# Two transformer blocks and two hybrid layers: inputs and output laid out by the host, x and the first weights loaded by pieces, and both heads' score banks filled in turn

## The chip, the cores and the metric

The kernel runs on one core of a Trainium2 chip. The metric is device time in microseconds (us), less is better. TensorE does matrix products and transposes, VectorE (DVE) and ScalarE (ACT) the elementwise work, GpSimd (POOL) little, and DMA transfers are issued from the queues of SyncE (SP) and ScalarE.

## What is computed

The input is x (256 tokens of 1024 features) and a memory of 256 tokens. A first model of two blocks is followed by a second one of two layers, all in float32. The first model, cut to its core:

```python
for i in range(DEPTH):                       # 2
    kvm = mem @ w_mem_kv[i]                  # 4 memory heads of 64
    if i % 2 == 0:
        proj = x @ w_in_swa[0]               # 12 heads, 3 key heads, window in chunks of 64
        self_out = swa_sink_attention(rope(q), rope(k), v, attn_sinks[0])
    else:
        proj = x @ w_in_fox[0]               # 12 heads, causal, bias cum[q] - cum[k]
        self_out = forgetting_attention(q, k, v, log_sigmoid(f_logit + b_forget[0]))
    cross_out = memory_attention(qc, km, vm)
    mix = concatenate([self_out, cross_out]) @ w_out[i]
    x = layer_norm(DN_ALPHA * x + mix, ln_attn_g[i], ln_attn_b[i])
    ffn = swiglu(x, ...) if i % 2 == 0 else moe_swiglu(x, ...)   # 8 experts, top 2
    x = layer_norm(DN_ALPHA * x + ffn, ln_ffn_g[i], ln_ffn_b[i])
```

The second model puts 16 meta tokens in front of the result and runs two layers. Each has a mixer (a gated delta rule with short convolutions beside an attention whose keys an indexer selects, then gates and an output product) and a convolutional gated MLP with D_FF 2816. The result is the 256 tokens without the meta tokens.

## The kernel before

Activations stand feature-major: partition = feature within a block of 128, then 8 blocks, then tokens. Every float32 number in the large products is cut into a high and a low part, and a product is three matmuls: high weight by high x (L228), high weight by low x (L229), low weight by high x (L230); L236 to L238 are the same with tokens on the output's partitions, L879 to L881 and L905 to L907 those of the experts. `linear` (L196) goes over groups of weight rows, `load_w` (L168) gets one: `fetch` (L165) puts a DMA of up to 1 MB on SP's queue into one of five buffers `raw`, ScalarE copies the high part `wh` (L179), VectorE subtracts for the low part `wl` (L182). The weights lie in memory as in the reference, so a transfer reads, for each partition, several strided rows.

The order within an engine's queue is fixed when the program is built, by a planner which goes by the order of the program text and by its own costs; each engine takes its queue strictly in that order.

At the start `consts` (L246) loads the constants `cst` by two DMAs on ScalarE's queue; `layer0` (L514) loads x token-major (`load_T`, L313: two DMAs of 512 KB on SP) and turns it (`turn`, L321): 16 transposes on TensorE (L327), a copy to float32 on VectorE (L331), the high part on ScalarE (L332), the low part on VectorE (L333). `rope1` (L335) makes the tables of sines; the rotation itself is a product with a constant matrix (L540). `vectors` (L259) loads the small vectors (gains, biases, convolution weights) row-wise by many DMAs on ScalarE's queue and turns them by TensorE (L278, L292, L303). `mem_tokens` (L488) loads and turns the memory like x.

`attend` (L421) handles two blocks b of two heads h at a time, in two halves t of the queries. For each t and h it takes one of two `sc` banks (each a PSUM bank); for each b a function `extra` puts a mask or bias into it (layer 0: L573, a product over 2 rows; layer 1: L667, a product over 44 rows with the cumulated gates, and L670, the causal mask), and the product of queries and keys over 64 rows is added (L434). A product with float32 operands is two records in the trace. Then the softmax: a maximum (L438) on VectorE, small operations, an exponential on ScalarE (L445) for each b, a scaling on VectorE (L453). The probabilities are transposed (L464), copied (L469 on ScalarE, L471 on VectorE) and multiplied with the values (L478); there the heads of a block write the two halves of the output's partitions, first all key tiles of one head, then those of the other. Head h=0 stands in partitions 0 to 63 of the queries and keys, h=1 in 64 to 127.

`moe` (L700) runs the router and 8 experts; a loop for tokens over the capacity follows it. `meta` (L955) loads the 16 meta tokens token-major and transposes them (L960). `consts2` (L926) loads the constants of the second model, among them `dtb` and `nA` (four small DMAs on SP, L947 and L948), and takes the exponential of the latter (L949), in ScalarE's queue beside the squares (L382) for the last norm of the first model. `gates` (L1224) loads 16 columns of w_in_2 as `ws` by two DMAs on SP. The last linear is the MLP's, with `ev` (L1093) adding its result to the stream h (L1094); then `store` (L963) transposes h (L970), copies it (L972, L974) and writes it by two DMAs of 512 KB (L975).

Of the kernel before, what the change touches and what calls it, by code (L numbers as in the profile page):

```python
# [105 lines left out]

class Kern:
# [88 lines left out]
    def linear(self, xs, w, c0, c, blocks, T, evac, tokmajor=(), accs=None, raws=None):  # L196
# [7 lines left out]
        wv = w.rearrange("(k p) c -> p k c", p=128)  # L204
# [12 lines left out]
        for k0, n in gs:  # L217
            wh, wl = self.load_w(wv[:, k0:k0 + n, ds(c0, c)], n, c)
# [39 lines left out]

    def vectors(self):  # L259
# [6 lines left out]
        I = self.i  # L266
        rows1 = [("ln_attn_g", 16), ("ln_attn_b", 16), ("ln_ffn_g", 16), ("ln_ffn_b", 16),
                 ("norm_mix_2", 16), ("norm_ffn_2", 16), ("b_gate_2", 32)]
        self.v = {}
        r = self.ap_.tile([128, T2], F, tag="sq", name="rows", bufs=2)[:, :128]  # L270
        o = 0
        vt = self.cp.tile([128, 128], F, name="vec1")
        for name, m in rows1:
            nc.scalar.dma_start(r[o:o + m, :], I[name].rearrange("l (k p) -> (l k) p", p=128))
            self.v[name] = vt[:, o:o + m].rearrange("p (l k) -> p l k", l=2)
            o += m
        p = self.pt()
        nc.tensor.transpose(p[:, :128], r, self.ident)  # L278
        nc.vector.tensor_copy(vt, p[:, :128])
# [3 lines left out]
        self.vn, self.convw, self.convf = {}, [], []  # L283
        r = self.ap_.tile([128, T2], F, tag="sq", name="rows", bufs=2)[:, :128]
        nc.vector.memset(r, 0.0)
        nc.scalar.dma_start(r[:96], I["conv_a_2"].rearrange("l i (k p) -> (l i k) p", p=128))
        for i, name in enumerate(("a_out_norm_2", "q_norm_2", "k_norm_2")):
            nc.scalar.dma_start(r[96 + 2 * i:98 + 2 * i], I[name])
        nc.scalar.dma_start(r[102:104, :64], I["kidx_norm_2"])
        vt = self.cp.tile([128, 128], F, name="vec2")  # L290
        p = self.pt()
        nc.tensor.transpose(p[:, :128], r, self.ident)  # L292
        nc.vector.tensor_copy(vt, p[:, :128])
        cv = vt[:, :96].rearrange("p (l i k) -> p l i k", l=2, i=4)
        self.convw = [cv[:, l] for l in range(2)]
        for i, name in enumerate(("a_out_norm_2", "q_norm_2", "k_norm_2", "kidx_norm_2")):
            self.vn[name] = vt[:, 96 + 2 * i:98 + 2 * i]
        vt = self.cp.tile([128, 2, 66], F, name="vec3")
        for l in range(2):
            r = self.ap_.tile([128, T2], F, tag="sq", name="rows", bufs=2)[:, :128]  # L300
            nc.scalar.dma_start(r[:66], I["conv_ffn_2"][l].rearrange("i (k p) -> (i k) p", p=128))
            p = self.pt()
            nc.tensor.transpose(p[:, :66], r[:66], self.ident[:66, :66])  # L303
            nc.vector.tensor_copy(vt[:, l], p[:, :66])
            self.convf.append(vt[:, l].rearrange("p (i k) -> p i k", i=3))
        self.sinks = self.cp.tile([128, 12], F, name="sinks")
        nc.scalar.dma_start(self.sinks, I["attn_sinks"].to_broadcast([128, 12]))
        self.brout = self.cp.tile([128, 8], F, name="brout")
        nc.scalar.dma_start(self.brout, I["b_router"].to_broadcast([128, 8]))
        self.bforg = self.cp.tile([12, 1], F, name="bforg")  # L310
        nc.scalar.dma_start(self.bforg, I["b_forget"].rearrange("o h -> h o"))

    def load_T(self, pool, src, name):  # L313
# [3 lines left out]
        for t in range(2):  # L317
            nc.sync.dma_start(raw[:, ds(t * D, D)], src[ds(t * 128, 128), :])
        return [raw[:, :D], raw[:, D:]]

    def turn(self, toks, xT, xh, xl):  # L321
        nc = self.nc
        for t, a in enumerate(toks):
            for g in range(2):
                p = self.pt()
                for b in range(4):
                    nc.tensor.transpose(p[:, ds(b * 128, 128)], a[:, ds((g * 4 + b) * 128, 128)], self.ident)  # L327
                pv = p.rearrange("p (b t) -> p b t", b=4)
                o = (slice(None), slice(g * 4, g * 4 + 4), ds(t * 128, 128))
                if xT is not None:  # L330
                    nc.vector.tensor_copy(xT[o], pv)  # L331
                nc.scalar.activation(xh[o], pv, AF.Copy)  # L332
                nc.vector.tensor_tensor(xl[o], pv, xh[o].bitcast(F), op=OP.subtract)  # L333
# [87 lines left out]
    def attend(self, pool, qs, ks, vs, outs, nk, extra=None, sink=None):  # L421
# [33 lines left out]
        for b in range(2):  # L455
# [32 lines left out]
    def mem_tokens(self, pool):  # L488
        toks = self.load_T(pool, self.i["mem"][0], "memt")
        m = self.pair(S)  # L490
        self.turn(toks, None, *m)
# [24 lines left out]
    def layer0(self):  # L516
# [3 lines left out]
        with tc.tile_pool(name="l0", bufs=1) as pool:  # L520
            toks = self.load_T(pool, I["x"][0], "xt")
            self.turn(toks, x, xh, xl)
# [6 lines left out]
            w = I["w_in_swa"][0]  # L529
# [84 lines left out]
    def layer1(self, x, xh, xl):  # L614
        nc, I, tc = self.nc, self.i, self.tc
        with tc.tile_pool(name="l1", bufs=1) as pool:
# [6 lines left out]
            wf = pool.tile([128, KB, 12], F, name="wf")  # L623
            nc.scalar.dma_start(wf, w[:, 2560:2572].rearrange("(k p) c -> p k c", p=128))
# [36 lines left out]
            for b0 in range(0, 6, 2):  # L661
# [4 lines left out]
                def extra(t, b, h, p, n):  # L666
                    nc.tensor.matmul(p, fselr[h * 64:h * 64 + 44, ds((2 * (b0 + b) + h) * 128, 128)],  # L667
# [1013 lines left out]
```

## Time and profile before

| | us |
|---|---|
| median of three runs | 2384.94 |
| lowest and highest | 2368.7, 2387.02 |
| the profiled execution | 2384.18 |
| its span | 2382.4 |

The profile is of one execution. Its times are within the span; 1.8 us lie around the span. An engine's queue is in order, so an instruction that waits holds all behind it. "PEclk" is the mean granted clock of TensorE, 1.00 being 2.4 GHz and 0.50 being 1.2 GHz. The ends of matmuls are modelled: two neighbours overlap by some hundredths of a microsecond as they are shown, and starts are the safer reading.

### The profile page before, as it was taken

How to read it: one execution, taken by the hardware profiler on the slowest of the kernel's cores; microseconds unless marked ns; L12 is line 12 of the kernel's file. 1: busy time of each engine (PE TensorE's matmuls, PEld its weight loads, DVE VectorE, ACT ScalarE, POOL GpSimd, SP SyncE). 2: the span in 40 equal slices, each digit the busy share in tenths (PEclk: the TensorE clock that was granted, in tenths of full speed). 3: DMA queues.
4: the chain of work that ended last, by engine and by line, in shares of the span. 5: the costliest groups of instructions: out<-in, count | busy, mean ns of one | idle time of the engine just before them, and what ended most of it. 6: DMA issues, size and time to landing. Idle time of an engine off the chain costs nothing. (4 is left out here: it accounts for less than half of the span.)

```text
span 2382.4 us, 37173 instructions
## 1 busy us (share of the span) xinstructions
PE 2296.6 (96%) x15054; PEld 2042.5 (86%) x15054; DVE 1695.8 (71%) x2645; ACT 1325.8 (56%) x1840; POOL 65.3 (3%) x110
## 2 busy tenths in 40 slices
PE   7989998998999999999999979999999999999999
PEld 7779998776888888888887768889999989899999
DVE  6565546546898888888888766776876565858764
ACT  4445435335776767767677565454554463555543
POOL 0000000000000000000000010000100000000000
PEclk9899998978999999999999979999999989999999
DMA  7225554334999999999999542224555522244653
GB/s 245 96 89 162 184 186 132 105 95 151 360 357 325 349 348 347 334 359 352 324 361 353 192 129 76 86 74 166 163 173 171 162 76 84 77 143 158 195 176 125
DMA packets 296260, 478.94 MB, mean 201 GB/s; under 512 B 14800, under 2 KB 160060, under 8 KB 296082
## 3 DMA queue, kind: packets, MB, share of 16 engines
q1 hardware_dynamic: 292224, 474.82, 58.6%
q8 instruction: 120, 1.97, 0.3%
q10 hardware_dynamic: 3714, 1.55, 0.3%
q14 instruction: 58, 0.48, 0.1%
q0 software_dynamic: 144, 0.13, 0.0%
HBM read 475.55 MB, written 1.05 MB: 200 GB/s over the span
## 5 line engine op out<-in xcount | busy, mean ns | idle before, releaser
L182 DVE TENSOR_TENSOR wl<-raw,wh 128x1024 fp32r<-128x1024 f32 (+2 forms) x565 | 882.4, 1573 | 295.9 <-ACT wh L179 293.8
L179 ACT ACTIVATE wh<-raw 128x1024 fp32r<-128x1024 f32 (+2 forms) x565 | 744.0, 1332 | 421.5 <-PE acc L229 248.4
L228 PE MATMUL acc<-xh,wh 128*128 128x272 f32 (+2 forms) x2224 | 645.2, 293 | 3.9 <-ACT qk L1120 1.8
L229 PE MATMUL acc<-xl,wh 128*128 128x272 f32 (+2 forms) x2224 | 646.6, 292 | 1.4 <-DVE xl L1043 1.1
L230 PE MATMUL acc<-xh,wl 128*128 128x272 f32 (+2 forms) x2224 | 644.2, 291 | 1.4 <-DVE wl L182 1.4
L228 PEld LDWEIGHTS acc<-xh,wh 128*128 128x128 f32 x2224 | 425.8, 193 | 9.9 <-ACT qk L1120 2.2
L229 PEld LDWEIGHTS acc<-xl,wh 128*128 128x128 f32 x2224 | 425.9, 192 | 8.1 <-issue 3.6
L230 PEld LDWEIGHTS acc<-xh,wl 128*128 128x128 f32 x2224 | 425.9, 192 | 4.1 <-DVE wl L182 2.1
L881 PE MATMUL acc<-wl,xe 128*128 128x512 f32 (+1 forms) x768 | 289.5, 378 | 3.0 <-DVE wl L182 3.0
L879 PE MATMUL acc<-wh,xe 128*128 128x512 f32 (+1 forms) x768 | 289.6, 377 | 0.0
L880 PE MATMUL acc<-wh,xe 128*128 128x512 f32 (+1 forms) x768 | 288.7, 376 | 0.0
L182 DVE TENSOR_TENSOR wl<-rawxl,wh 128x2048 fp32r<-128x2048 f32 x73 | 166.3, 2289 | 17.9 <-ACT wh L179 17.6
L881 PEld LDWEIGHTS acc<-wl,xe 128*128 128x128 f32 x768 | 144.3, 188 | 31.6 <-DVE wl L182 5.1
L879 PEld LDWEIGHTS acc<-wh,xe 128*128 128x128 f32 x768 | 144.8, 189 | 26.7
L880 PEld LDWEIGHTS acc<-wh,xe 128*128 128x128 f32 x768 | 144.3, 188 | 26.2
L179 ACT ACTIVATE wh<-rawxl 128x2048 fp32r<-128x2048 f32 x73 | 139.6, 1916 | 32.1 <-PE acc L906 15.6
L228 PE MATMUL acc<-gh,wh 128*128 128x256 f32 (+1 forms) x528 | 150.3, 285 | 0.0
L229 PE MATMUL acc<-gl,wh 128*128 128x256 f32 (+1 forms) x528 | 150.2, 285 | 0.0
L230 PE MATMUL acc<-gh,wl 128*128 128x256 f32 (+1 forms) x528 | 150.1, 284 | 0.0
L906 PE MATMUL acc<-wh,egl 128*128 128x512 f32 x352 | 139.4, 396 | 0.0
L905 PE MATMUL acc<-wh,egh 128*128 128x512 f32 x352 | 139.1, 395 | 0.0
L907 PE MATMUL acc<-wl,egh 128*128 128x512 f32 x352 | 132.8, 396 | 0.0
(554 smaller groups left out, 3022.7 us busy)
## 6 DMA issues: line engine op xcount, KB each, us to landing
raw<-in_w_exp_in_dram SPq DMA_DIRECT2D x125, 1024.0 KB, 6.0
raw<-in_w_exp_out_dram SPq DMA_DIRECT2D x64, 1024.0 KB, 7.0
rawxl<-in_w_exp_in_dram SPq DMA_DIRECT2D x49, 1024.0 KB, 5.8
raw<-in_w_up_dram SPq DMA_DIRECT2D x44, 1024.0 KB, 5.2
rawxl<-in_w_exp_out_dram SPq DMA_DIRECT2D x24, 1024.0 KB, 7.5
raw<-in_w_in_dram SPq DMA_DIRECT2D x24, 1024.0 KB, 5.4
raw<-in_w_ffn_in_dram SPq DMA_DIRECT2D x22, 1024.0 KB, 5.0
raw<-in_w_out_dram SPq DMA_DIRECT2D x16, 1024.0 KB, 5.0
```

The source lines that it names most:

```text
L179: nc.scalar.activation(h[:, o], raw[:, o], AF.Copy)
L182: nc.vector.tensor_tensor(l[:, o], raw[:, o], h[:, o].bitcast(F), op=OP.subtract)
L228: nc.tensor.matmul(o, f(wh[:, j]), xh[:, k], start=st, stop=False)
L229: nc.tensor.matmul(o, f(wh[:, j]), xl[:, k], start=False, stop=False)
L230: nc.tensor.matmul(o, f(wl[:, j]), xh[:, k], start=False, stop=sp)
L879: nc.tensor.matmul(a, xe[0][:, k], wh[:, q], start=k == 0, stop=False)
L880: nc.tensor.matmul(a, xe[1][:, k], wh[:, q], start=False, stop=False)
L881: nc.tensor.matmul(a, xe[0][:, k], wl[:, q], start=False, stop=k == KB - 1)
L905: nc.tensor.matmul(ys[h], gh[:, k], wh[:, q, o], start=k == 0, stop=False)
L906: nc.tensor.matmul(ys[h], gl[:, k], wh[:, q, o], start=False, stop=False)
L907: nc.tensor.matmul(ys[h], gh[:, k], wl[:, q, o], start=False, stop=k == FB - 1)
```

## The change

It rearranges what the host hands over and the order of some work; the products are the same.

- Weights: each group of rows that `load_w` asks for lies as one contiguous block in memory, partition by partition (`Packed`); the DMA has one run for each partition. The host makes the blocks.
- x and mem: handed over feature-major. x is loaded in four pieces of two blocks, with the two halves of the first weight tile in turn (`load_x`), and its parts are cut piece by piece; mem is one fetch and two cuts. The transposes go. The constants `cst` go to SP's queue, behind x and the first weights, as one DMA.
- Small vectors: one array made by the host, one DMA; the transposes go. Later parts of it (`late`) hold the forget gate's weights, the router's, the meta tokens and `ws`, each loaded by one DMA on ScalarE's queue where it is used. `dtb` and the logarithms for `nA` are in the part that is loaded at the start.
- `attend`: both heads' banks are taken together, `extra` is called once for each t and h with a product over both blocks where it can be, and the score products go through the blocks with the heads in turn. The products with v go through the key tiles with the heads in turn.
- Output: feature-major. Each block of 128 features (128 KB) is stored right after its last addition, straight from h; the host turns the result.

```diff
+class Packed:
...
+    def tile(self, l, k0, n, c0, c):
+        key = (k0, n, c0, c)
+        if key not in self.places:
+            self.places[key] = self.used
+            self.used += 128 * n * c
...
+        return self.ap[l, o:o + 128 * n * c].rearrange("o (p x) -> (o p) x", p=128)
...
     def fetch(self, src, kb, c, raw=None):
         raw = self.raw() if raw is None else raw
-        self.nc.sync.dma_start(raw[:, :kb * c].rearrange("p (k c) -> p k c", k=kb), src)
+        self.nc.sync.dma_start(raw[:, :kb * c], src)
...
-            wh, wl = self.load_w(wv[:, k0:k0 + n, ds(c0, c)], n, c)
+            wh, wl = self.load_w(w(k0, n, c0, c), n, c)
...
-        nc.scalar.dma_start(t[:, :128], self.cst_d[:, :128])
-        nc.scalar.dma_start(t[:, 128:], self.cst_d[:, 128:n])
+        self.cst = t
...
+        vt = self.cp.tile([128, n], F, name="vec")
+        nc.scalar.dma_start(vt, self.i["vec"][:, :n])
...
+    def late(self, pool, name):
+        a, w = self.i["off"][name]
+        t = pool.tile([128, w], F, name=name)
+        self.nc.scalar.dma_start(t, self.i["vec"][:, ds(a, w)])
+        return t.rearrange("p (k c) -> p k c", k=KB)
+
+    def load_x(self, x, xh, xl, w):
         nc = self.nc
         raw = self.raw()
...
+        for k in range(0, KB, 2):
+            o = slice(k, k + 2)
+            nc.sync.dma_start(x[:, o], self.i["x"][:, ds(k * S, 2 * S)].rearrange("p (k t) -> p k t", k=2))
+            if k < 4:
+                q = ds(k * 512, 1024)
+                nc.sync.dma_start(raw[:, q], w[:, q])
+        self.ahead.append(raw)
+        for k in range(0, KB, 2):
+            o = slice(k, k + 2)
+            self.split(xh[:, o], xl[:, o], x[:, o])
+        nc.sync.dma_start(self.cst, self.cst_d[:, :self.cst.shape[1]])
...
-            for h in range(2):
-                p = self.sc()
-                pv = p[:, :2 * n].rearrange("p (b k) -> p b k", b=2)
-                sl = slice(h * 64, h * 64 + 64)
-                for b in range(2):
-                    started = extra(t, b, h, pv[:, b], n) if extra else False
-                    nc.tensor.matmul(pv[:, b], qs[b][sl, ds(t * 128, 128)], ks(b, h)[:, :n],
-                                     start=not started, stop=True)
+            pvs = [self.sc()[:, :2 * n].rearrange("p (b k) -> p b k", b=2) for _ in range(2)]
+            if extra:
+                for h in range(2):
+                    extra(t, h, pvs[h], n)
+            for b in range(2):
+                for h in range(2):
+                    sl = slice(h * 64, h * 64 + 64)
+                    nc.tensor.matmul(pvs[h][:, b], qs[b][sl, ds(t * 128, 128)], ks(b, h)[:, :n],
+                                     start=b == 0 and not extra, stop=b == 1, skip_group_check=True)
+            for h, pv in enumerate(pvs):
...
             o = self.pt()
-            for h in range(2):
-                for kt in range(2):
-                    c0, t = segs[kt]
-                    n = (2 - t) * 128
+            for kt in range(2):
+                c0, t = segs[kt]
+                n = (2 - t) * 128
+                for h in range(2):
...
-            def extra(t, b, h, p, n):
-                nc.tensor.matmul(p, hmb[:, :128], hmb[:, ds(128 + t * 256, n)], start=True, stop=False)
-                return True
+            def extra(t, h, p, n):
+                nc.tensor.matmul(p, hmb[:, :128], hmb[:, None, ds(128 + t * 256, n)].to_broadcast([2, 2, n]),
+                                 start=True, stop=False, skip_group_check=True)
...
+                def extra(t, h, p, n):
+                    for b in range(2):
+                        nc.tensor.matmul(p[:, b], fselr[h * 64:h * 64 + 44, ds((2 * (b0 + b) + h) * 128, 128)],
+                                         cum[h * 64:h * 64 + 44, :n],
+                                         start=b == 0, stop=False, skip_group_check=True)
+                    nc.tensor.matmul(p[:, :, ds(t * 128, 128)], self.identb,
+                                     self.causb[:, None, :].to_broadcast([128, 2, 128]),
+                                     start=False, stop=False, skip_group_check=True)
...
-            nc.sync.dma_start(self.dtb[:, l], I["dt_bias_2"][l:l + 1].to_broadcast([128, 4]))
-            nc.sync.dma_start(self.nA[:, l], I["a_log_2"][l:l + 1].to_broadcast([128, 4]))
-        nc.scalar.activation(self.nA, self.nA, AF.Exp)
+        nc.scalar.activation(self.nA, al, AF.Exp)
...
-                if not l:
+                if l:
+                    nc.sync.dma_start(self.out[:, ds(k * S, S)], h[:, k, NM:])
+                else:
                     self.ready(h, k, self.v["norm_mix_2"][:, 1])
...
-        nc.sync.dma_start(ws[:, :, 0:8], wv[:, :, 2048:2056])
-        nc.sync.dma_start(ws[:, :, 8:16], wv[:, :, 3400:3408])
+        ws = self.late(pool, f"ws{l}")
```

## Rows read from the trace of the kernel before

**Rows 1.** The page: TensorE's share of the span, and traffic in 40 slices.

```profile
PE 2296.6 (96%) x15054; PEld 2042.5 (86%) x15054; DVE 1695.8 (71%) x2645; ACT 1325.8 (56%) x1840; POOL 65.3 (3%) x110
...
GB/s 245 96 89 162 184 186 132 105 95 151 360 357 325 349 348 347 334 359 352 324 361 353 192 129 76 86 74 166 163 173 171 162 76 84 77 143 158 195 176 125
```

**Rows 2.** Stages: length, busy time (instructions) of each engine, PEclk, DMA share, GB/s.

```profile
58.00:76.00 18.00, 15.34 (x66) 11.13 (x64) 10.85 (x38) 8.75 (x23) 0.00 (x0) 0.62 0.51 175
76.00:141.00 65.00, 63.63 (x381) 46.71 (x380) 38.72 (x130) 28.33 (x89) 0.00 (x0) 0.97 0.20 66
...
477.00:506.00 29.00, 29.00 (x95) 18.88 (x93) 12.43 (x42) 10.13 (x31) 0.00 (x0) 0.53 0.02 6
...
600.00:1300.00 700.00, 697.03 (x3360) 574.63 (x3359) 609.39 (x393) 494.08 (x342) 0.00 (x0) 1.00 0.98 347
```

**Rows 3.** TensorE's waits, 600 to 1300 us: total, times, longest (us).

```profile
PE acc L881 <- DVE wl L182: 3.0, 5, 0.6
```

**Rows 4.** Timeline of the start: start and duration (us), engine, line, idle before.

```profile
11.53 1.06 ACT L179 ACTIVATE wh<-raw 128x1024 fp32r<-128x1024 f32 x1 [2.21 <-DMA raw<-in_w_in_swa_dram]
...
11.85 0.39 PE L573 MATMUL sc<-hmb 2*128 2x128 bf16 x2 [5.11 <-DVE hmb L528]
...
14.99 1.22 PE L228 MATMUL acc<-xh,wh 128*128 128x256 f32 x4 [0.56 <-ACT xh L332]
```

**Rows 5.** Stages of five microseconds at the start; traffic (GB/s) is last.

```profile
0.00:5.00 5.00, 0.23 (x1) 0.23 (x2) 0.37 (x3) 0.00 (x0) 0.20 (x4) 1.00 0.62 199
5.00:10.00 5.00, 1.74 (x8) 1.33 (x7) 1.43 (x3) 2.48 (x3) 0.00 (x0) 1.00 0.94 296
```

**Rows 6.** Timeline of TensorE near 60 us.

```profile
61.51 0.56 PE L303 MATMUL pt<-cst,rows 66*128 66x66 f32 x2 [1.60 <-DVE sm L441]
63.12 1.97 PE L327 MATMUL pt<-cst,raw 128*128 128x128 f32 x8 [1.05 <-DVE vec L304]
...
65.34 1.22 PE L434 MATMUL sc<-kT,qT 64*128 64x256 f32 x2
```

**Rows 7.** Timeline of TensorE in layer 0's attention and memory attention.

```profile
91.74 0.23 PE L573 MATMUL sc<-hmb 2*128 2x128 bf16 x1
91.89 0.48 PE L434 MATMUL sc<-kT,qT 64*128 64x128 f32 x2
...
92.96 0.28 PE L573 MATMUL sc<-hmb 2*128 2x256 bf16 x1
93.17 0.70 PE L434 MATMUL sc<-kT,qT 64*128 64x256 f32 x2
...
97.27 1.35 PE L478 MATMUL pt<-pT,v 128*64 128x256 f32 x8
...
112.84 0.88 PE L478 MATMUL pt<-pT,v 128*64 128x256 f32 x8
...
119.11 1.13 PE L434 MATMUL sc<-kmT,qm 64*128 64x256 f32 x4
```

**Rows 8.** Timelines of layer 1's attention, and the sparse layer's index scores (L1511).

```profile
474.42 0.38 PE L667 MATMUL sc<-cumhl,fselr 44*128 44x256 f32 x1
...
476.53 0.69 DVE L438 TENSOR_REDUCE sm<-sc 128x2 f32<-128x512 f32 x1 [1.25 <-PE sc L434]
...
477.49 0.89 PE L434 MATMUL sc<-kT,qT 64*128 64x256 f32 x2
...
477.74 0.47 ACT L445 ACTIVATE pe<-sc,sm 128x256 f32<-128x256 f32 x1 [3.18 <-DVE sm L442]
...
1523.96 1.23 PE L1511 MATMUL sc<-ikd,bi 64*128 64x256 f32 x8
```

**Rows 9.** Timeline of TensorE in the first model's last norm.

```profile
1377.36 0.80 PE L401 MATMUL pt<-cst,sq 128*128 128x1 f32 x3 [2.95 <-ACT sq L382]
```

**Rows 10.** Timeline of the tail.

```profile
2375.42 0.42 DVE L1094 TENSOR_TENSOR xa<-xa,acc 128x256 f32<-128x256 f32 x1 [1.74 <-PE acc L230]
...
2377.06 1.79 SPq L975 DMA_DIRECT2D out_dram<-raw  x2
```

More of the change, by code (lines that the diff above doesn't have):

```diff
@@ L104, in make_consts, with __init__, array, __getitem__ @@
     return np.concatenate(parts, 1), off
+class Packed:
+    def __init__(self, nc, name, a):
+        self.a = np.asarray(a).reshape(-1, a.shape[-2], a.shape[-1])
+        self.size = self.a.shape[1] * self.a.shape[2]
+        self.name = f"in_{name}_dram"
+        self.ap = nc.dram_tensor(self.name, (self.a.shape[0], self.size), F, kind="ExternalInput").ap()
+        self.places, self.used = {}, 0
+    def tile(self, l, k0, n, c0, c):
[3 more added lines that the diff above has]
+            self.used += 128 * n * c
+            assert self.used <= self.size
+        o = self.places[key]
+        l = ds(l, 1) if isinstance(l, int) else l
+        return self.ap[l, o:o + 128 * n * c].rearrange("o (p x) -> (o p) x", p=128)
+    def array(self):
+        out = np.zeros((self.a.shape[0], self.size), np.float32)
+        for (k0, n, c0, c), o in self.places.items():
+            t = self.a[:, k0 * 128:(k0 + n) * 128, c0:c0 + c].reshape(-1, n, 128, c)
+            out[:, o:o + 128 * n * c] = t.transpose(0, 2, 1, 3).reshape(-1, 128 * n * c)
+        return out
+    def __getitem__(self, l):
+        return lambda *a: self.tile(l, *a)
@@ new lines, in make_vectors @@
+def make_vectors(i):
+    blocks = lambda a: np.asarray(a).reshape(-1, 128).T
+    rows = lambda a: np.tile(np.asarray(a).reshape(1, -1), (128, 1))
+    cut = lambda w: np.asarray(w).reshape(8, 128, -1).transpose(1, 0, 2).reshape(128, -1)
+    low = lambda a: np.concatenate([a, np.zeros((128 - a.shape[0], a.shape[1]), np.float32)], 0)
+    w2 = np.asarray(i["w_in_2"])
+    cols = {k: blocks(i[k]) for k in ("ln_attn_g", "ln_attn_b", "ln_ffn_g", "ln_ffn_b", "norm_mix_2", "norm_ffn_2",
+                                      "b_gate_2", "conv_a_2", "conv_ffn_2", "a_out_norm_2", "q_norm_2", "k_norm_2")}
+    cols["kidx_norm_2"] = low(np.asarray(i["kidx_norm_2"]).T)
+    for k in ("attn_sinks", "b_router", "dt_bias_2", "a_log_2"):
+        cols[k] = rows(i[k])
+    cols["b_forget"] = low(np.asarray(i["b_forget"]).T)
+    cols["meta"] = cut(np.asarray(i["meta_tokens_2"]).T)
+    cols["wf"] = cut(np.asarray(i["w_in_fox"])[0, :, 2560:])
+    cols["wr"] = cut(np.asarray(i["w_router"])[0])
+    for l in range(2):
+        cols[f"ws{l}"] = cut(np.concatenate([w2[l][:, 2048:2056], w2[l][:, 3400:3408]], 1))
+    off, n = {}, 0
+    for k, v in cols.items():
+        off[k] = (n, v.shape[1])
+        n += v.shape[1]
+    return np.ascontiguousarray(np.concatenate(list(cols.values()), 1)), off
@@ L264, in vectors @@
         nc.vector.tensor_copy(self.causb, self.c["causal"])
[L266 to L276, printed above, removed]
@@ L298, in vectors @@
[L298 to L305, printed above, removed]
@@ L306, in vectors @@
[L306 to L313, printed above, removed]
+        cv = v["conv_a_2"].rearrange("p (l i k) -> p l i k", l=2, i=4)
@@ L488, in mem_tokens @@
     def mem_tokens(self, pool):
-        toks = self.load_T(pool, self.i["mem"][0], "memt")
+        raw = self.fetch(self.i["mem"], KB, S)
         m = self.pair(S)
-        self.turn(toks, None, *m)
+        raw = raw.rearrange("p (k t) -> p k t", k=KB)
+        for k in range(0, KB, 4):
+            self.split(*(a[:, k:k + 4] for a in (*m, raw)))
         self.kmT, self.vm = [], []
@@ L621, in layer1 @@
             v = pool.tile([128, 2, 768], F, name="v")
-            wf = pool.tile([128, KB, 12], F, name="wf")
-            nc.scalar.dma_start(wf, w[:, 2560:2572].rearrange("(k p) c -> p k c", p=128))
+            wf = self.late(pool, "wf")
             wfh = pool.tile([128, KB, 12], R, name="wfh")
@@ L705, in moe @@
             raws = [None] * 5 + [self.idle(t) for t in ("xl", "xa")] + [self.pair_y(pool, F).rearrange("p a c -> p (a c)")]
-            self.ahead = [self.fetch(*a, r) for a, r in zip(self.in_tiles(I["w_exp_in"][0, :1]), raws)]
+            self.ahead = [self.fetch(*a, r) for a, r in zip(self.in_tiles(I["w_exp_in"][0]), raws)]
             self.spare = True
-            wr = pool.tile([128, KB, 8], F, name="wr")
-            nc.scalar.dma_start(wr, I["w_router"][0].rearrange("(k p) c -> p k c", p=128))
+            wr = self.late(pool, "wr")
             w2 = pool.tile([128, KB, 16], R, name="wr2")
@@ L773, in moe @@
                     y = h[:, :, NM:]
-                    self.meta(h, self.pair_y(pool, F)[:, 0])
-                self.expert_out(pool, gT, now, I["w_exp_out"][0, e:e + 1], y, None if e else x)
+                    nc.vector.tensor_copy(h[:, :, :NM], self.late(pool, "meta"))
+                self.expert_out(pool, gT, now, I["w_exp_out"][e], y, None if e else x)
             q = self.pt()[:, :8]
@@ L1671, in build @@
             k.run()
+    for name in _WEIGHTS:
+        arrays[aps[name].name] = aps[name].array()
     return nc, arrays
```

122 lines of the change are left out of this document (34 added, 88 removed).

## The prediction

> **What bounds the kernel now.** I read the page's first part, then the table of stages, then TensorE's waits, and only then single instructions. TensorE is busy 2296.6 us, 96% of the span [rows 1]. In the table of stages the long stretch 600 to 1300 us holds 697.0 us of matmul in 700, although the DMA share is 0.98 there [rows 2]; the waits say the same from the other side, TensorE waiting 3.0 us in all, for VectorE's splits and never for a transfer [rows 3]. So a faster transfer has nothing to give there: the cover is the matmuls themselves. Time can come only from work that TensorE no longer does, from the few spots where it stands, and from its clock. The stretches that the change touches are the start, 58 to 141 (layer 0's attention), 430 to 513 (layer 1's), the spot near 1377, and the tail. In two of them the granted clock is low: mean 0.62 in 58 to 76, 0.53 in 477 to 506 [rows 2], that is almost wholly at 1.2 GHz.
>
> **The start.** Before, TensorE transposes x, stands 5.11 us behind the first mask product L573 (it had been put ahead in the queue and waits for a cast), transposes again, and begins the first real product at 14.99 us [rows 4]. After, x arrives transposed, in four pieces of 256 KB with two halves of the first weights (512 KB each) between. The first ten microseconds moved 199 and 296 GB/s [rows 5], so the first piece and half (768 KB) are there at about 4.3 us, and all 2 MB at 5 + 1.0/0.296 = 8.5 us. Splitting a half weight of 1024 columns takes ScalarE 1.06 us [rows 4], a piece of x of 512 columns by that about 0.6. If the first half weight is split right behind the first piece, the first product starts near 6.2 us, 8.8 earlier. If ScalarE, whose queue is in order, does all four pieces of x first, it starts at 8.5 + 0.6 + 1.06 = 10.2 us, 4.8 earlier, and less if the clock rises as late as now. What is then late next is the constants, which now travel behind x: the rope needs them by the end of the first linear. I take 6 us, bounds 3 and 9.
>
> **Vectors and memory tokens, 58 to 71.** L278, L292, L303 and the 16 transposes of mem go. From 59.91 (61.51 less its wait of 1.60) to 65.1 (63.12 and 1.97) TensorE does only these [rows 6]; of the other eight transposes of mem, two groups of four, I count as much again as the eight took, 1.97: 7.2 us. The stretch lies at the lower clock too, and what remains in it would be quicker without: a pair of 256-key score records takes 1.22 us there against 0.70 later [rows 6, 7], three pairs give 1.6 us, and the linear that follows up to 75 us, also at half clock, about 1.9. 11 us if the clock stays up, 5 if the softmax fills the hole; I take 9. On the queues, eleven small DMAs of ScalarE become one; nothing waits behind them.
>
> **Attention, layer 0.** Before, for each head and block: a mask product, then two records of a score product. With 256 keys these are shown with 0.28 and 0.70 us, with 128 with 0.23 and 0.48; the starts (92.96 and 93.17, 91.74 and 91.89) show that about 0.07 of each lies under the next, so 0.21 + 0.63 and 0.16 + 0.41 [rows 7], each four times a half. So an attend has 4 x 0.84 + 4 x 0.58 = 5.7 us of scores. The change lets two heads, in rows 0 to 63 and 64 to 127 of the array, follow each other, with one mask product per head for both blocks. That such neighbours overlap is in the trace: in the sparse layer eight records of 256 columns, heads in turn, span 1.23 us [rows 8], where four of memory's, one head's, take 1.13 [rows 7]. After: 2 x 0.31 + 1.15 at 256 keys, 2 x 0.21 + 0.5 at 128: 2.7 us, saving 3.0 an attend, 9 for three. Memory's scores: four records and four again, 2.1, against 1.15; 0.95 twice is 1.9. The products with v go to two column halves: eight records took 1.35 us in one order and 0.88 in another [rows 7], and others are cut in two by other work; I take 0.6 less for each of six and 0.75 for memory's two: 5.1. Sum 16 us.
>
> **Attention, layer 1.** One half with 256 keys runs from 474.42 to 478.38 (477.49 and 0.89) [rows 8], about 3.7 us without the lower clock at its end. After: four cumulative products of 0.21, two mask products of about 0.2, 1.15 of scores: 2.4. So 1.3 less, and as the 128-key half shrinks by the same share (0.9), 2.2 an attend, 6.6 for three; with memory and v as above (1.9 + 5.1) 13.6 us. Together 29.5 us of TensorE time. I count two thirds, 20, because TensorE's order is fixed beforehand: VectorE has 38.7 us of work in 65 already [rows 2], and where TensorE arrives early it stands. Both ends: 5, if the softmax decides (below); 37, if the 29 us at clock 0.53 shrink with it as well.
>
> The Trainium skill ("TensorEngine Tiling (Array Packing)", Key Properties) says that changing the tiling mode drains TensorE. The rows agree in so far as a mask product holds TensorE 0.21 us with 256 columns and 0.16 with 128, so about 0.1 is fixed [rows 7]. By that rule eight changes for each half become two, and an estimated 0.3 us a half more goes, 2 us a layer, which I leave out of the sum.
>
> **Small parts.** The decay constants come from a tile long loaded: TensorE waits 2.95 us at 1377.36 for the squares of ScalarE [rows 9], in whose queue the exponential of these constants, and so their DMA, stood in front; I take 2 us, bounds 0 and the whole wait. The eight small meta transposes go: at somewhat under the fixed 0.1 us of a small product, 0.6 us, and nothing waits for them. The small gate weights move from SP to ScalarE's queue: one issue of about 0.4 us there, hidden under idle time of ScalarE unless its tile's space is still in use; 0. The tail: before, the last addition ends at 2375.84, transposes and copies follow, the issue of the second 512 KB store ends at 2378.85 [rows 10], and the span ends 3.5 us later. After, eight stores of 128 KB, of which only the last stands behind the last addition: its issue (0.4 us) ends near 2376.3, and 3.3 us for the smaller transfer make 2379.6; 2.8 us earlier, bounds 2 and 4.
>
> **Layout of the weights.** Contiguous pieces replace strided rows. No stage in which the traffic is heavy waits for it [rows 3]: 0, the cover being 697 us of matmul in 700. If that cover were not there, see the second rival.
>
> **Sum.** 6 + 9 + 20 + 2 + 0.6 + 2.8 = 40.4 us from the profiled execution's 2384.18 us (span 2382.4 and 1.8 around it, 0.8 below the median of 2384.94): 2344 us. Lower ends of the gains: 3 + 5 + 5 + 0 + 0 + 2 = 15, giving 2369; upper ends: 9 + 11 + 37 + 3 + 0.6 + 4 = 65, giving 2319.
>
> **Rivals.**
> *The softmax takes the gain back.* Both heads' banks are now taken at once, and there are only two, so the next half's scores wait until both softmaxes are through; before, one head could go ahead. A reduction of 256 keys takes 0.69 us and each of four exponentials 0.47 [rows 8], so a round cannot be under about 0.9 + 1.4 + 1.9 = 4 us, and eight rounds a layer make 32 us. The linears between them are as long, which speaks against it; the fixed order speaks for it. Attention then gives 3 instead of 20: 2361 us. The Trainium skill ("TensorEngine Tiling (Array Packing)", PSUM Bottleneck) warns of just this: packing speeds up TensorE, not the emptying of its banks. The trace cannot show it yet, because the heads run serially in it.
>
> *The layout speeds the experts.* DMA share 0.98 could mean that the transfers set the pace. Then the stage would rise from 347 GB/s to the best slice's 361 [rows 1, 2], 700 x (1 - 347/361) = 27 us: 2317. Against it: TensorE's waits of 3.0 us. The Trainium skill ("DMA: Bandwidth & Descriptors", Where 436 GB/s comes from) puts the limit for one core near 358 GB/s; by that figure it would be an estimated 22 us, and the stage already stands at the limit.
>
> *Slower: the clock.* TensorE with less to do in attention stands more often, and the clock falls, as it did in 477 to 506 and 58 to 76. Work at 1.2 GHz costs double: from some 40 us of full-clock work that drops to half, everything gained is gone. The stretch of layer 0 is 65 us long now [rows 2] and that of layer 1 (430 to 506) some ten longer, of it 29 at half clock already; less what is saved, about 90 us of full-clock work are left in them; with 60 of these at half clock, 2344 + 60 = 2404 us. For it: two such stretches in the trace. Against it: the linears between the softmaxes stay, and one cause of the fall, the transposes at 61, goes.
>
> *The heads don't overlap.* If the new neighbours run serially, only the fewer mask products (half an attend's 0.1 us fixed parts, 3 us in all) remain of attention: 2344 + 17 = 2361. The sparse layer's records speak against it [rows 8].
>
> **Chances.** Forecast 0.60, softmax 0.18, layout 0.07, clock 0.06, no overlap 0.09. One per cent (about 24 us, what a measurement here can tell) lies at 2361, where two rivals end; I give a third of them to faster. Faster: 0.60 + 0.07 + (0.18 + 0.09) / 3 = 0.76; slower 0.05 of the clock's 0.06; same 0.19. The range 2315 to 2368 holds all but the clock and the worst ends.
>
> **What would show it.** The first product of the first linear before 11 us; no transposes near 60, and the clock at 1.0 there; score products of the two heads starting at almost one time; 76 to 141 shorter by 10 or more; 600 to 1300 with the same matmuls in the same time at a lower DMA share; the end within 4 us of the last addition. Wrong would be: TensorE's waits on the softmax grown by over 15 us, an expert stage shorter than now, or a granted clock under 0.7 over attention.

## The result, and the profile after

The changed kernel takes 2352.12 us (four runs, 2348.41 to 2355.69) against 2383.62 us of the kernel before beside it: a ratio of 0.9885, interval 0.9848 to 0.9922. That is 31.5 us less, where 40.4 were forecast (2344, range 2315 to 2368). All eight runs of the changed kernel, and the 48 of the kernel before that stand beside the experiments below, give medians of 2352.1 and 2378.5 us, 26 us apart.

First the page after, its lines on the engines, the clock and the traffic.

```profile
span 2350.5 us, 36949 instructions
...
PE 2266.5 (96%) x14970; PEld 2018.7 (86%) x14970; DVE 1691.3 (72%) x2632; ACT 1324.2 (56%) x1836; POOL 63.1 (3%) x110
...
PEclk9799998979999999999999879999999989999999
...
DMA packets 70032, 478.91 MB, mean 204 GB/s; under 512 B 7960, under 2 KB 10906, under 8 KB 13792
```

The traffic is the same 479 MB, in 70032 packets where there were 296260, so the layout did arrive at the DMA engines. TensorE is 96% busy as before, with 30 us less of busy time [rows 1].

The table of stages (length, busy time of PE, PEld, DVE, ACT and POOL, PEclk, DMA share, GB/s):

```profile
53.00:76.00 23.00, 21.01 (x163) 18.99 (x161) 14.77 (x40) 12.27 (x31) 0.00 (x0) 1.00 0.43 157
76.00:100.00 24.00, 23.89 (x76) 14.14 (x75) 11.43 (x52) 8.29 (x35) 0.00 (x0) 0.51 0.13 45
100.00:132.00 32.00, 31.07 (x180) 20.65 (x179) 20.47 (x70) 13.49 (x44) 0.00 (x0) 1.00 0.10 33
132.00:414.00 282.00, 269.62 (x2162) 264.74 (x2162) 158.54 (x246) 132.46 (x198) 11.68 (x10) 0.96 0.46 160
414.00:484.00 70.00, 67.57 (x429) 48.95 (x428) 43.95 (x126) 31.23 (x92) 0.00 (x0) 1.00 0.26 91
...
590.00:1300.00 710.00, 707.01 (x3428) 583.77 (x3426) 618.07 (x397) 501.97 (x349) 0.00 (x0) 1.00 0.92 348
```

The experts' stretch is as dense as before, 707.0 us of matmul in 710, at a DMA share of 0.92 instead of 0.98 [rows 2]. What moved is the clock: layer 1's attention (414 to 484) now holds 1.00, where 477 to 506 stood at 0.53 [rows 2]; layer 0's is low for longer, 0.51 over 24 us (76 to 100) where 0.62 stood over 18.

To see where time went I compare the starts of the same work in the two traces, one execution each (2384.18 and 2352.28 us). VectorE cuts 640 groups of weights in the same order in both (L182, now L240). The lead of the changed kernel is 6.4 us at the 17th cut (59.7 and 53.3 us), 10.1 behind layer 0's attention (144.5 and 134.4), 11.1 ahead of layer 1's (425.9 and 414.9), 32.4 behind it (579.5 and 547.2), 33.2 through all experts (1351.1 and 1317.9), 28.4 from the middle of the hybrid layers to the last cut. The tail brings 3.5 more, 31.9 in all. Attention of layer 1 alone made two thirds of the gain; layer 0's, with the vectors and mem, made 4 us.

The rows of after that answer to [rows 4] and [rows 10], the first product and the last addition:

```profile
8.03 0.58 PE L285 MATMUL acc<-xh,wh 128*128 128x256 f32 x1
...
2347.01 0.42 DVE L1099 TENSOR_TENSOR xa<-xa,acc 128x256 f32<-128x256 f32 x1 [1.73 <-PE acc L287]
```

The first product starts at 8.03 instead of 14.99 us. The span ends 3.1 us behind the last addition (2347.43 to 2350.5), where it was 6.6 (2375.84 to 2382.4).

And the rows that answer to [rows 7], layer 0's scores (64*128 is 64 rows of the array in use; x4 are two products of two records):

```profile
63.49 0.71 PE L464 MATMUL sc<-kT,qT 64*128 64x128 f32 x8
...
69.84 0.37 PE L605 MATMUL sc<-hmb 2*128 2x512 bf16 x1
70.14 1.13 PE L464 MATMUL sc<-kT,qT 64*128 64x256 f32 x4
71.20 0.39 PE L605 MATMUL sc<-hmb 2*128 2x512 bf16 x1
71.51 1.13 PE L464 MATMUL sc<-kT,qT 64*128 64x256 f32 x4
...
75.24 0.26 PE L605 MATMUL sc<-hmb 2*128 2x256 bf16 x1 [1.99 <-ACT pe L476]
75.43 0.71 PE L464 MATMUL sc<-kT,qT 64*128 64x128 f32 x4
```

Only the first group, x8 in 0.71 us, has the heads in turn. From then on the planner has put one head's mask and all four records ahead of the other head's: 1.13 us each, just as serial as before. The written order is not the order in the queue. In layer 1 more of it is left: 21 of 64 score records start within 0.03 us of the next record, against 10 before; in layer 0 they are 4 against 2, and 24 in the run below that keeps the turns.

**A measure that the clock hardly moves.** The kernel before gave anything from 2366.2 to 2387.4 us. Each run records its span and its mean granted clock. One run of 2367.63 us has a span of 2365.9 at 0.971, one of 2387.26 a span near 2385.5 at 0.963: both products are 2297. Over 48 runs span times clock lies within 2293.8 and 2301.9. (The clock is given to three places, worth 1.2 us of the product.) So nearly all of this kernel's spread is time at 1.2 GHz, which is twice one minus the mean clock, times the span: 128 to 177 us here. The product says what a change did apart from it. It isn't a time: a wait while the clock is low counts half in it. Before it is 2297.6 in the median, after 2278.4: of the 26 us between the medians about 19 are work and waits, some 7 the clock. One run falls out of this picture: of the ten of e_attendonly below, one of 2383.83 us has a mean clock of 0.910, so 429 us at 1.2 GHz and a product of 2168, and yet is only some 18 us longer than the others. Why is not shown; I use the product only between runs of nearly the same clock (0.959 to 0.973).

### The profile page after: what moved, and what is told of

Same layout as the page of the kernel before. It is cut to its first block, busy times and chain, and to the rows that moved or that the text cites. A ratio compares the mean times of both kernels' runs of the same rounds, so it can differ in the third digit from the quotient of the medians.

```text
span 2350.5 us, 36949 instructions
## 1 busy us (share of the span) xinstructions
PE 2266.5 (96%) x14970; PEld 2018.7 (86%) x14970; DVE 1691.3 (72%) x2632; ACT 1324.2 (56%) x1836; POOL 63.1 (3%) x110
## 2 busy tenths in 40 slices
DMA packets 70032, 478.91 MB, mean 204 GB/s; under 512 B 7960, under 2 KB 10906, under 8 KB 13792
## 5 line engine op out<-in xcount | busy, mean ns | idle before, releaser
L240 DVE TENSOR_TENSOR wl<-raw,wh 128x1024 fp32r<-128x1024 f32 (+2 forms) x565 | 882.5, 1573 | 299.4 <-ACT wh L237 297.4
L240 DVE TENSOR_TENSOR wl<-rawxl,wh 128x2048 fp32r<-128x2048 f32 x73 | 166.4, 2289 | 17.9 <-ACT wh L237 17.6
```

Of the source, the lines that this page charges most:

```text
L240: nc.vector.tensor_tensor(l[:, o], raw[:, o], h[:, o].bitcast(F), op=OP.subtract)
```

## The experiments

| kernel | runs | median us | ratio to before | span x clock |
|---|---|---|---|---|
| changed, again (e_after) | 4 | 2352.1 | 0.9889 (0.9846 to 0.9932) | 2279.1 |
| old attention (e_oldattend) | 10 | 2380.2 | 0.9994 (0.9967 to 1.0021) | 2288.1 |
| before, attention alone (e_attendonly) | 10 | 2365.2 | 0.9949 (0.9921 to 0.9977) | 2289.3 |
| heads serial, new masks (e_masksonly) | 4 | 2355.9 | 0.9898 (0.9863 to 0.9934) | 2281.6 |
| before, new masks alone (e_masksbefore) | 8 | 2360.4 | 0.9931 (0.9906 to 0.9956) | 2288.2 |
| heads held in turn (e_turns) | 4 | 2358.3 | 0.9907 (0.9870 to 0.9944) | 2282.6 |
| strided weights (e_strided) | 4 | 2352.3 | 0.9876 (0.9844 to 0.9908) | 2275.3 |
| x in one piece (e_xwhole) | 5 | 2358.8 | 0.9916 (0.9887 to 0.9945) | 2283.2 |
| old vectors and mem (e_oldvec) | 5 | 2358.6 | 0.9921 (0.9895 to 0.9946) | 2283.8 |
| old decay constants (e_oldna) | 4 | 2347.9 | 0.9875 (0.9833 to 0.9917) | 2276.6 |
| gate weights on SP (e_ws_sp) | 4 | 2358.2 | 0.9907 (0.9871 to 0.9943) | 2275.7 |
| one store at the end (e_storeend) | 6 | 2354.6 | 0.9914 (0.9884 to 0.9943) | 2280.5 |

The runs stand in four groups, each beside runs of the kernel before, whose medians are 2378.0 to 2381.3 us and whose median products 2296.0 to 2300.1. The changed kernel stands beside e_oldna and e_storeend alone, and e_strided, which takes as long, beside e_turns, e_oldattend and e_attendonly. In the group of e_masksonly, e_ws_sp, e_xwhole and e_oldvec there is no changed kernel. Differences of 3 to 7 us between two rows lie within the intervals of their ratios; where I read them, I give the product or the trace beside them.

For attention there is a second measure, worked out from each trace: the time from each record of scores, masks, transposes and value products to TensorE's next record, less idle time, times the clock granted just then ("held" below, layer 0 + layer 1). Before: 40.1 + 44.9 us; after: 35.0 + 36.5.

### Attention, undone and alone

```diff
 e_oldattend: the changed kernel with attend, extra and the value products of the kernel before
 e_attendonly: the kernel before with those of the changed kernel
```

> The changed kernel with attention as before (banks, masks, score and value products head after head). Theory: the TensorE time of attention goes back up by 13.5 us at full clock (5.1 in layer 0, 8.4 in layer 1), so about 2352 + 13 = 2365 us, and up to 9 more if layer 1 falls to 1.2 GHz again as it did before (2374 us). Rival (the gain of layer 1 came from the clock alone, which follows the new start and not attention): layer 1 stays at full clock and the time is 2352 to 2358 us.

> The kernel before with only attention changed. Theory: 13.5 us of TensorE time at full clock, and 5 to 9 us more from the part of layer 1 that ran at 1.2 GHz: 2384 - 14 to 2384 - 22, so 2362 to 2370 us. Rival (clock alone, by the new start): no more than 5 us, 2379 to 2384 us.

Without its new attention the changed kernel takes 2380.2 us, hardly less than the kernel before: attention carries 28 us of the time, and 10 of span times clock; held time is 41.5 + 44.7 there. Put into the kernel before, it gives 13 to 16 us (2365.2), and 8 by span times clock. So the gains don't add up: with the old attention, the new start, vectors and tail together show 1 us (2381.3 beside it), though 9.7 by span times clock (2297.8 to 2288.1). The clock takes the difference: 176 us at 1.2 GHz in the median of e_oldattend, 162 in the kernel before beside it. Stages of layer 1 in the profile of the old attention in the new kernel:

```profile
414.00:460.00 46.00, 46.00 (x259) 33.70 (x257) 25.56 (x68) 17.83 (x50) 0.00 (x0) 1.00 0.26 94
460.00:500.00 40.00, 40.00 (x161) 26.89 (x161) 19.58 (x58) 13.38 (x41) 0.00 (x0) 0.66 0.09 29
```

With the new start, layout and vectors in place, layer 1 falls to 0.66 again as soon as attention is the old one. So the rival (the clock follows the start) falls. The theory's upper figure of 2374 was still 6 us short; nine of the ten runs have more time at 1.2 GHz (171 to 195 us) than any of the changed kernel's eight (131 to 155), the tenth, of 2367.69 us, has 151.

### Which part of attention: masks or turns

```diff
 e_masksonly (in the changed kernel), e_masksbefore (in the kernel before) (extract, against the kernel before; extra is the changed kernel's):
             for h in range(2):
...
+                if extra:
+                    extra(t, h, pv, n)
                 for b in range(2):
-                    started = extra(t, b, h, pv[:, b], n) if extra else False
                     nc.tensor.matmul(pv[:, b], qs[b][sl, ds(t * 128, 128)], ks(b, h)[:, :n],
...
```

> The changed kernel with the heads one after the other again in scores and value products, but with the changed mask products (one over both blocks for a head). Theory (masks are the smaller part, the turns of the heads the larger, and the turns keep the clock up in layer 1): about 4 of attention's 14 to 15 us of TensorE time at full clock remain saved, so 2380 - 4 = 2376 us, and layer 1 falls to 1.2 GHz for over 20 us. Rival (fewer mask products, which change the array's rows from 2 or 44 to 64 and back, are the main gain): 2352 to 2362 us with layer 1 at full clock.

> The kernel before with the changed mask products alone (one for a head over both blocks, bias products together), heads one after the other, no change of layout, start or tail. Theory (the masks are the larger part of what attention gained and keep layer 1 at 2.4 GHz): span times mean granted clock about 6 us under the kernel before's 2297, and the time 2362 to 2370 us, near the 2365 of the kernel before with all of attention changed. Rival (the masks help only together with the new start and layout): 2375 to 2384 us with layer 1 at 1.2 GHz for over 20 us.

I had expected the turns to be the larger part. It is the masks. With heads serial and only the masks changed, the time is 2355.9 us, 4 above the changed kernel; in the kernel before, this edit alone gives 2360.4, 18 us less, no less a gain than all of the new attention there (2365.2, in another group). Held time falls from 40.1 + 44.9 to 38.2 + 39.6 us, so 7 us are TensorE's own. Of layer 1's 5.3 us, 2.9 are the cumulative products (7.0 to 4.1) and 1.2 the causal masks (3.8 to 2.6). There are 24 cumulative products in both, but now two of a head stand together: 0.36 us for two with 128 keys, where one held TensorE 0.21 to 0.26 before. And some overlap with the other head's scores: in the timeline of e_masksbefore the second pair starts 0.01 us behind a score record, and five of the 24 hold TensorE less than 0.09 us in this way.

```profile
424.12 0.43 PE L669 MATMUL sc<-cumhl,fselr 44*128 44x128 f32 x2
424.48 0.28 PE L672 MATMUL sc<-causb,identb 128*128 128x256 bf16 x1
424.70 0.37 PE L435 MATMUL sc<-kT,qT 64*128 64x128 f32 x1
424.71 0.44 PE L669 MATMUL sc<-cumhl,fselr 44*128 44x128 f32 x2
```

Span times clock falls by 9 us (2297.6 to 2288.2), or by 12 against the kernel before beside it (2300.1). The rest of the 18 is the clock, which in layer 1 of the profiled run stays at 1.00:

```profile
420.00:480.00 60.00, 59.96 (x371) 44.84 (x369) 40.70 (x120) 28.02 (x88) 0.00 (x0) 1.00 0.23 77
```

Among the profiles, the two with the old masks, before and e_oldattend, have 27 us and more at 1.2 GHz in layer 1's attention; those with the new masks have none there or one stretch of 7 us at its end. That is one profile for each kernel, two for the changed one. The old masks don't force the fall: 13 of the 48 runs of the kernel before, between 2366 and 2375 us, have 128 to 142 us at 1.2 GHz in all, no more than the runs of e_masksbefore (137 to 146). Where these 13 had it no profile shows.

The written turns on top of the masks bring held time down by another 6 us (77.3 to 71.5 in the changed kernel, 77.8 to 71.6 in the kernel before). The median is 4 us shorter with them in the one and 5 longer in the other, so a gain in time is not shown.

### The heads really in turn

```diff
 e_turns: an edge from each product to the next (order alone, no wait), so that the planner keeps the written order
+    def in_turn(self, chain):
+        for a, b in zip(chain, chain[1:]):
+            self.tc.add_manual_dep(b.ins, a.ins.name, ...
```

> The changed kernel, with edges in the program that hold the planner to the written order: mask products of both heads first, then the four score products with the heads in turn, and the four value products with the heads in turn. Theory (the planner undid the turns, TensorE bounds attention): every score group of 256 keys spans about 1.15 us instead of 2.1, some 5 us of TensorE time less in layer 0 and 3 in layer 1 beyond the changed kernel, 2352 - 8 = about 2344 us, if the clock does not fall more. Rival (the softmax bounds attention as soon as both banks are taken at once): TensorE's waits on VectorE and ScalarE in attention, now 2.8 us in layer 0, grow by more than the 8 us saved, 2352 to 2360 us.

The overlap is real: four products of the two heads in 1.14 us, where after needed 1.13 for two. But the next half then waits for both softmaxes. A timeline and waits (total, times, longest) of TensorE in layer 0, e_turns:

```profile
72.37 0.38 PE L614 MATMUL sc<-hmb 2*128 2x512 bf16 x1
72.69 1.14 PE L470 MATMUL sc<-kT,qT 64*128 64x256 f32 x8
...
78.56 0.37 PE L614 MATMUL sc<-hmb 2*128 2x256 bf16 x1 [4.49 <-ACT pe L483]
...
PE sc L614 <- ACT pe L483: 6.5, 2, 4.5
PE pt L502 <- DVE pe L491: 4.4, 5, 2.7
PE sc L470 <- ACT pe L483: 0.7, 2, 0.4
```

and the same waits of the changed kernel:

```profile
PE sc L605 <- ACT pe L476: 2.0, 1, 2.0
PE pt L509 <- DVE pT L502: 0.8, 1, 0.8
```

Held time falls by 6.1 us (30.5 + 34.9), waits on the softmax in layer 0 grow by 9, and the kernel is 6 us slower than the changed one and than e_strided beside it; by span times clock 4 us more than the changed one. Of the theory the first half holds (the planner had undone the turns); the rival holds too (the softmax bounds, once they are kept), and the time follows it. By breaking the turns the planner kept TensorE fed.

### The layout, the start, the vectors

```diff
 e_strided: weights as in the reference, transfers strided as before
 e_xwhole:  x by one DMA of 1 MB, then the first weights by one of 1 MB
 e_oldvec:  small vectors and mem row-wise, transposed on TensorE as before
```

> The changed kernel with the weights laid out as in the reference again, so that a transfer reads strided rows; all else as changed. Theory (the layout is worth nothing, since TensorE sets the pace of the experts): 2352 us, within 4, and the same 700 us for the experts' stretch at a DMA share of 0.98. Rival (the layout brought part of the gain, by the first weights or by the experts): 5 us or more above, 2357 to 2370 us.

> The changed kernel with x as one transfer of 1 MB and the first weights as one of 1 MB behind it, instead of pieces in turn. Theory (the pieces bring the first product forward): first product near 10 us instead of 8.0, and 2 to 3 us at the end of the first linears, 2354 to 2355 us. Rival (the rope's constants and tables set the first stage anyway): no change at 50 us, 2352.

> The changed kernel with the small vectors and the memory tokens loaded row-wise and transposed on TensorE again, as before. Theory (TensorE time counts one for one, half clock included): 7 to 11 us, 2359 to 2363 us. Rival (the transposes hide in the waits for the first softmax, and only the clock changes): 2350 to 2356 us.

e_strided is at 2352.3 us: the layout of the weights is worth nothing here, and its product, 2275 against 2278, speaks for no gain either. Its experts take as long as the changed kernel's at a larger DMA share:

```profile
590.00:1300.00 710.00, 707.07 (x3429) 584.42 (x3428) 618.16 (x400) 502.58 (x349) 0.00 (x0) 1.00 0.97 348
```

For x in one piece my 2 to 3 us were too few: the first product starts at 12.81 us, and the lead lost is 5.4 us at the 17th cut; in the median it is 6.7, in the product 4.8. ScalarE shows why; e_xwhole's first rows:

```profile
0.75 0.68 SPq L351 DMA_DIRECT2D xa<-in_x_dram  x1
1.48 0.64 SPq L352 DMA_DIRECT2D raw<-in_w_in_swa_dram  x1
8.61 2.19 ACT L218 ACTIVATE xh<-xa 128x512 fp32r<-128x512 f32 x4 [4.71 <-DMA xa<-in_x_dram]
11.70 2.00 ACT L237 ACTIVATE wh<-raw 128x1024 fp32r<-128x1024 f32 x2 [0.91 <-DMA raw<-in_w_in_swa_dram]
```

So x is there only shortly before 8.61 us, and the weights before 11.70. By the traffic some 1.9 MB had been moved at 8.6 us, though x is 1 MB: what was issued behind it ran beside it. The cuts of both, 2.2 and 1.1 us, lie behind that; in pieces the cuts run under the transfers. The old vectors cost 6.5 us in the median and 5.4 in the product, just under the 7 to 11 expected; of the five runs (2353.4 to 2360.4) one alone lies where the rival, that they hide, had them.

### Small parts

```diff
 e_oldna:    dtb and nA by four DMAs on SP, as before
 e_ws_sp:    self.late(pool, f"ws{l}") on SP's queue
 e_storeend: one store of 1 MB behind the last addition
 e_after:    no edit
```

> The changed kernel with the decay constants loaded by four small transfers on SP again. Theory (ScalarE's exponential waits for them in front of the squares): TensorE's moments of the last norm take about 14.9 us again instead of 11.0, and the time is 2 to 4 us longer, 2354 to 2356 us. Rival (the stretch up to 1500 us gives it back anyway, since it is bound elsewhere): 2352 us within 2.

> The changed kernel with the small gate weights of the two hybrid layers loaded from SP's queue instead of ScalarE's. Theory (the 8 us that the changed kernel gives back between the last norm of the first model and 1500 us come from ScalarE's queue, in which this transfer and its cut now stand): 2352 - 5 = 2347 us, and no stretch at 1.2 GHz near 1400. Rival (the planner's order and the clock, not this transfer): 2350 to 2354 us and the same stretch.

> The changed kernel with the whole output stored by one transfer of 1 MB behind the last addition instead of eight of 128 KB each behind its own. Theory (the tail is the last transfer's issue and landing, and a larger one lands later): the end comes 2 to 3 us later than now after the last addition, 2354 to 2355 us. Rival (a transfer's fixed part is nearly all of it): within 1 us, so of the 3.5 us won at the tail nearly all came from the transposes and copies.

> The changed kernel once more, beside the runs below and on their chip. If run-to-run spread is the clock's, span times mean granted clock stays within 2276 to 2281 us as in its four first runs, and the time moves between 2348 and 2358 us with the clock.

e_oldna is the surprise: with the waiting transfer back it has the lowest median of the study, 2347.9 us (2345.5 to 2349.1), 4 under the changed one, whose four runs beside it took 2349.0 to 2354.4. That is hardly clear of the spread, but a loss it is not. The moments of the last norm do take 14.1 us again (1332.51 to 1346.60) against 11.0 (1332.06 to 1343.07), but what comes next takes part of it back. First after, then e_oldna:

```profile
1347.27 0.98 PE L436 MATMUL sc<-cst,sm 128*128 128x128 f32 x3 [4.02 <-DVE sm L998]
```

```profile
1343.95 2.72 PE L429 MATMUL pt<-cst,sq 128*128 128x1 f32 x12 [1.76 <-ACT sq L410]
...
1348.70 1.19 PE L436 MATMUL sc<-cst,sm 128*128 128x128 f32 x4 [1.92 <-DVE sm L1001]
```

Counted from the start of the norm (1332.06 and 1332.51) the next product starts after 15.2 and 16.2 us, so of 3.1 us one is left there. Behind it the changed kernel gives more back up to 1500 us; which order of the planner, and how much by the clock (products of 2278 and 2277), is open. The gate weights on SP did not bring the 5 us that I expected: 2358.2, 6 slower at a lower product, with 163 us at 1.2 GHz in the median against some 145. That explanation of the loss near 1400 falls, and what stands in its place is not settled. One store at the end costs 2.5 us in the median and 2.7 in the trace, whose span ends 5.8 us behind the last addition (2346.31 to 2352.1), with an issue of 0.64 us: the size counts, so of the 3.5 us of the tail most came with the small pieces. e_after repeats the changed kernel: 2352.1, products 2275.8 to 2279.7.

## Why the prediction was right or wrong, step by step

**What bounds the kernel.** Right: TensorE, in every stage that the change touches, and its clock. The layout's 0 is confirmed by e_strided, and with it the rival of faster experts falls: at 348 GB/s TensorE waited 3.0 us in the stage, and not for a transfer. The limit near 358 GB/s that the prediction took for that rival from the Trainium skill ("DMA: Bandwidth & Descriptors", Where 436 GB/s comes from) is none here: between 10 and 20 us the changed kernel moves 415 to 434 GB/s.

**The start.** 6 us taken; the lead is 6.4 us at the 17th cut, and e_xwhole gives 5.4 there for the pieces alone. The first product at 8.03 lies between the two bounds of 6.2 and 10.2. ScalarE cut the weights right behind the first piece of x, as the early bound had it, but from 6.78 us and not from about 5.1 (6.2 less the cut of 1.06): the weights came later than the traffic of the kernel before had let me expect.

**Vectors and mem.** 9 taken; e_oldvec shows 6.5, 5.4 by span times clock. The term was too large. Of the 7.2 us of "TensorE time" 2.65 were waits [rows 6], and TensorE's waits between 53 and 145 us did not go: 4.1 us in the trace before, 3.5 after. The transposes themselves come to 2.5 us of held time, double at 1.2 GHz. The rest was to come from the clock, and layer 0's clock got worse (0.51 over 24 us) instead of better.

**Attention.** 29.5 us of TensorE time were counted, two thirds of which, 20, were to show. The profile has 13.5 us less held time (5.1 and 8.4), and the stage-by-stage lead shows some 21 us in layer 1 and hardly any in layer 0. The sum is near, the reasons are not, and that the time fell into the range is in part luck: layer 0 gave next to nothing of its 16 us in the lead, and some 13 of layer 1's 21 came from a clock that stood in the upper bound alone. The step that failed is that the written order would be the executed one: the planner put the heads one after the other again, in layer 0 nearly everywhere. By held time scores and masks fell by 3.8 us there where 9 were counted, memory's scores by nothing and value products by 1.6 where 1.9 and 5.1 were; in layer 1 by 6.2, 0.5 and 2.3 for 6.6, 1.9 and 5.1. The term that was mis-sized is the masks. I had 0.1 us fixed in each, so 3 us in all, in the rival of no overlap; they measure 18 us in the kernel before, 9 to 12 by span times clock and the rest by the clock. The rule that I left out of the sum, that a change of the tiling mode drains TensorE (the Trainium skill, "TensorEngine Tiling (Array Packing)", Key Properties), points this way and was put at 4 us in two layers; the held times of masks and cumulative products fall by 5.2 (e_masksbefore). That this is a drain is argued, no run shows it; for five of the 24 cumulative products the trace shows an overlap with scores instead.

**The softmax rival.** It didn't decide this kernel (2.8 us of waits in layer 0), because the turns were not kept. Where they are, in e_turns, it does: the warning of the Trainium skill ("TensorEngine Tiling (Array Packing)", PSUM Bottleneck) agrees with the 6.5 us there, in which a mask product waits until the exponential has read its bank. The 4.4 us are transposes that wait for scaled probabilities, which is the softmax too, but not the bank.

**The clock rival.** As a rival I had it as a loss only; the gain stood in attention's upper bound of 37. Layer 0 has that loss, layer 1 the opposite gain, about 13 us of its lead (29 us at 0.53 went). On balance the clock gave 7 us.

**Small parts.** The moments' 2 us were 3.9 where they were sought and 1.9 at the next product (17.1 us behind the norm's start before, 15.2 after), but e_oldna, which gives them back, is no slower. The meta transposes 0.8 for 0.6 (the lead grows from 32.4 to 33.2 in the experts). The tail 3.5 for 2.8. Not foreseen: 5 us given back between the experts and 1500 us.

## What to carry to other kernels

In a kernel whose order a planner makes, an edit that lives from two products standing together has to be looked for in the queue; and if a shared bank makes them wait for one another, keeping them together can cost more than it saves. Small mask products between score products held TensorE longer here than their columns account for, 0.16 us with 128 columns, 0.21 with 256 and some 0.3 with 512: merge them first, it was a few lines here and most of the gain. Before crediting an edit, compare span times mean granted clock of all runs: here the same kernel varied by 21 us, and that product by 8.

## What the runs showed that was not expected

The kernel before varies from 2366 to 2387 us with its mean granted clock between 0.973 and 0.963, while span times clock varies by 8. In the profiles a few merged mask products go with 1.00 instead of 0.53 over nearly 30 us of layer 1's attention; the same masks left layer 0 at half clock for up to 24 us in several profiles. What the throttle goes by is not shown by these runs. An edit that takes a wait of 3 us away need not make a kernel faster (the changed kernel against e_oldna, whose median is 4 us lower).
